# Dense expert scaling: the x input in two loads instead of three, and the first store tied to its own tile alone

## The chip, the cores and the metric

The kernel runs on one core of one Trainium2 chip. The metric is the device time in microseconds (us) of one execution; lower is better. Beside it stands the profile of one execution, whose span runs from the first to the last instruction of the core.

## What is computed

The inputs are `x`, 8 x 256 x 512 in float32 (4.19 MB), and `gate_weights`, 8 x 256 x 8 in float32. Each token's eight gate weights are divided by their sum, and each token's 512 values are multiplied by each of the eight results. The output is 8 x 256 x 8 x 512 in float32 (33.55 MB).

```python
gate_weights = gate_weights / (np.sum(gate_weights, axis=-1, keepdims=True) + 1e-8)
output = x[:, :, None, :] * gate_weights[:, :, :, None]
```

## The kernel before, in words

The 2048 tokens lie on 128 partitions, 16 consecutive tokens to a partition (`J` = 16), so that a token number j from 0 to 15 stands for 128 tokens, one per partition. All of x is kept on the chip in `x_all`, 32 KB a partition; one token j is 2 KB of a partition's row.

**Loads.** `first_load` (line 67, SP's queue) brings tokens 0 to 3, 8 KB a partition. `gate_load` (line 68, ACT's queue) brings all gate weights. `body_load` (line 69, SP) brings tokens 4 to 12, 18 KB a partition. These three are moved ahead of the barrier at the entry of the program, to the front of their engines' instructions, by `issue_before_entry_barrier`. The tail load (line 73, SP) brings tokens 13 to 15, 6 KB a partition, and is issued after that barrier.

**Gates.** Four small DVE instructions (lines 78 to 81) make the normalised gates `gn`.

**Products.** The results go into `ring`, ten slots of 16 KB a partition, one token j with its eight experts to a slot. `CHUNKS` lists the five stores as (first token, number of tokens, first slot): tokens 0-1 in slots 0-1, tokens 2-4 in slots 2-4, tokens 5-7 in slots 5-7, tokens 8-11 in slots 0-3, tokens 12-15 in slots 6-9. Slots 0 to 3 and 6 to 7 are used twice, so tokens 8 and 9 wait for store 0, tokens 10 and 11 for store 1, and tokens 12 and 13 for store 2. For tokens 0 and 1 ACT does three of the eight experts (line 88) and DVE five (line 90), one instruction to an expert; token 2 is all ACT's; of token 3 ACT does two and DVE six; tokens 5, 8 and 12 are all ACT's; each of the other tokens is one DVE instruction over all eight experts (line 93).

**Stores.** Each chunk ends in one DMA on SP's queue (line 118), which waits for the instructions that fill its slots. An extra dependency (lines 121 to 129) makes the first store wait for `body_load` too.

**Order.** Each engine takes its own instructions in order. The order in which the tokens of an engine stand is made by the framework's scheduler when the program is built, from the dependencies; it need not be the order of the source. SP issues all x loads and stores in one queue, and each DMA is spread over 16 DMA engines, 8 of the 128 partition rows to an engine. Nine DMAs are issued in all: three loads of x, one of the gates, five stores.

Of the kernel before, what the change touches and what calls it, by code (L numbers as in the profile page):

```python
# [1 line left out]

# [4 lines left out]

SLOTS = 10
HEAD = 4
TAIL = 13  # L10
CHUNKS = ((0, 2, 0), (2, 3, 2), (5, 3, 5), (8, 4, 0), (12, 4, 6))


def issue_before_entry_barrier(nc, loads):
    names = [bi.ins.name for bi in loads]

    def move(nc):
        blocks = nc.main_func.blocks
        entry = blocks[0].instructions
        moved = []  # L20
        for block in blocks[1:]:
            for ins in list(block.instructions):
                if ins.name in names:
                    block.instructions.remove(ins)
                    moved.append(ins)
        assert sorted(i.name for i in moved) == sorted(names)
        for ins in reversed(moved):
            at = next(k for k, other in enumerate(entry) if other.engine == ins.engine)
            entry.insert(at, ins)

    nc.at_finalize(move)


@with_exitstack
def kernel(
    ctx: ExitStack,
    tc: tile.TileContext,
    x: bass.AP,
    gate_weights: bass.AP,
    out: bass.AP,  # L40
):
    nc = tc.nc
    P = 128

    B, S, D = x.shape
    E = gate_weights.shape[-1]
    J = B * S // P

    fp32 = mybir.dt.float32
    mult = mybir.AluOpType.mult  # L50

    x_v = x.flatten_outer_dims().rearrange("(p j) d -> p j d", p=P)
    g_v = gate_weights.flatten_outer_dims().rearrange("(p j) e -> p j e", p=P)
    out_v = out.rearrange("b s e d -> (b s) e d").rearrange(
        "(p j) e d -> p j e d", p=P
    )

    pool = ctx.enter_context(tc.tile_pool(name="pool", bufs=1))

    g_all = pool.tile([P, J, E], fp32)  # L60
    x_all = pool.tile([P, J, D], fp32)
    ring = pool.tile([P, SLOTS, E, D], fp32)
    gsum = pool.tile([P, J, 1], fp32)
    gn = pool.tile([P, J, E], fp32)
    warm = pool.tile([P, 1], fp32)

    first_load = nc.sync.dma_start(out=x_all[:, 0:HEAD, :], in_=x_v[:, 0:HEAD, :])  # L67
    gate_load = nc.scalar.dma_start(out=g_all, in_=g_v)
    body_load = nc.sync.dma_start(
        out=x_all[:, HEAD:TAIL, :], in_=x_v[:, HEAD:TAIL, :]  # L70
    )
    issue_before_entry_barrier(nc, [first_load, gate_load, body_load])
    nc.sync.dma_start(out=x_all[:, TAIL:J, :], in_=x_v[:, TAIL:J, :])

    nc.vector.memset(warm, 0.0)  # L75
    nc.scalar.copy(out=warm, in_=warm)  # L76

    nc.vector.reduce_sum(out=gsum, in_=g_all, axis=mybir.AxisListType.X)  # L78
    nc.vector.tensor_scalar_add(out=gsum, in0=gsum, scalar1=1e-8)  # L79
    nc.vector.reciprocal(out=gsum, in_=gsum)  # L80
    nc.vector.tensor_tensor(  # L81
        out=gn, in0=g_all, in1=gsum.to_broadcast([P, J, E]), op=mult
    )

    def scale_one(engine, j, e, slot):
        o_ap, s_ap = ring[:, slot, e, :], gn[:, j, e : e + 1]
        if engine is nc.scalar:
            nc.scalar.mul(out=o_ap, in_=x_all[:, j, :], mul=s_ap)  # L88
        else:
            nc.vector.tensor_scalar_mul(out=o_ap, in0=x_all[:, j, :], scalar1=s_ap)  # L90

    def scale_token(j, slot):
        nc.vector.tensor_tensor(  # L93
            out=ring[:, slot, :, :],
            in0=x_all[:, j : j + 1, :].to_broadcast([P, E, D]),
            in1=gn[:, j, :].unsqueeze(2).to_broadcast([P, E, D]),
            op=mult,
        )

    for j0, m, s0 in CHUNKS:  # L100
        for i in range(m):
            j, slot = j0 + i, s0 + i
            if j < 2:
                for e in range(E):
                    on_act = e < 3
                    scale_one(nc.scalar if on_act else nc.vector, j, e, slot)
            elif j == 2:
                for e in range(E):
                    scale_one(nc.scalar, j, e, slot)
            elif j == 3:  # L110
                for e in range(E):
                    scale_one(nc.scalar if e < 2 else nc.vector, j, e, slot)
            elif i == 0:
                for e in range(E):
                    scale_one(nc.scalar, j, e, slot)
            else:
                scale_token(j, slot)
        store = nc.sync.dma_start(  # L118
            out=out_v[:, j0 : j0 + m, :, :], in_=ring[:, s0 : s0 + m, :, :]
        )  # L120
        if j0 == 0:
            tc.add_manual_dep(
                store.ins,
                body_load.ins.name,
                mybir.DependencyInfo(
                    mybir.DependencyClass.Sync, mybir.DependencyReason.DATA
                ),
                reason="no store among the loads",
            )


# [1 line left out]
_INS = ['x', 'gate_weights']  # L133
_OUTS = [((8, 256, 8, 512), 'float32')]


# [23 lines left out]
```

## Time and profile before

| what | value |
|---|---|
| median of 4 runs | 92.37 us (92.28 to 92.44) |
| the profiled execution's own time | 92.29 us |
| its span, first to last instruction | 90.5 us |
| DVE busy | 46.6 us (51%), 30 instructions |
| ACT busy | 26.3 us (29%), 42 instructions |
| DMA | 37.81 MB: 4.26 read from HBM, 33.55 written; 418 GB/s over the span |
| ACT waited for stores (line 88) | 25.0 us, in two waits |
| DVE waited for stores (line 93) | 3.7 us, in one wait |

The profile gives for each engine how long it was busy and what ended its idle time. DMA instructions appear twice: as issue on the queue's engine (SPq is SP's), which takes 0.33 to 0.42 us, and as landing, the time from the issue until the data's semaphore has arrived. Of the stores, store 0 was issued at 10.62 us from the span's start, store 1 at 17.15, store 2 at 25.82, store 3 at 47.50 and store 4 at 56.19; they landed 11.5, 19.4, 25.2, 22.9 and 33.5 us after their issues. A rate in GB/s is the bytes of the DMA packets recorded in a stretch.

### The profile page before, as it was taken

What the parts mean: (1) busy time and instruction counts of PE and PEld (TensorE: products, weight loads), DVE (VectorE), ACT (ScalarE), POOL (GpSimd) and SP (SyncE); (2) the same over time, 40 slices, a digit from 0 to 9 for tenths busy, and PEclk for the clock granted to TensorE, in tenths of its full rate; (3) what the DMA queues carried; (4) which work ended last, traced back from release to release, by engine and by line L of the source; (5) the groups of instructions that cost most, each with busy time, mean ns of one, the idle gap of its engine ahead of it and who ended that gap; (6) DMA issues with size and microseconds to landing.
All of it is one profiled execution on the core that took longest, in us unless ns stands there. A gap on an engine that the chain in (4) does not pass through costs nothing.

```text
span 90.5 us, 140 instructions
## 1 busy us (share of the span) xinstructions
DVE 46.6 (51%) x30; ACT 26.3 (29%) x42; POOL 0.2 (0%) x4
## 2 busy tenths in 40 slices
DVE  0069999999999999999990395000000000000000
ACT  4229999995990000000000398000000000000000
POOL 0000000000000000000000000000000000000000
DMA  5999999999898889888988999999999982999990
GB/s 127 470 417 399 415 518 463 463 420 391 348 695 348 348 348 695 348 348 348 695 348 348 463 463 463 463 463 463 463 463 463 463 377 87 463 463 463 463 463 0
DMA packets 1296, 37.81 MB, mean 418 GB/s; under 512 B 144, under 2 KB 272, under 8 KB 400
## 3 DMA queue, kind: packets, MB, share of 16 engines
q1 hardware_dynamic: 1152, 37.75, 97.2%
q10 hardware_dynamic: 144, 0.07, 0.2%
HBM read 4.26 MB, written 33.55 MB: 418 GB/s over the span
## 4 chain that ended last, share of the span: by engine, by line
DMA 52%; ACT 9%; ACTq 1%; SPq 0%; issue 0%
DMA out_dram<-ring 41%; DMA x_all<-in_x_dram 11%; ACT ring L88 9%; ACTq L155 1%; SPq L67 0%; ACTq L88 0%; SPq L118 0%
## 5 line engine op out<-in xcount | busy, mean ns | idle before, releaser
L93 DVE TENSOR_TENSOR ring<-x_all,gn 128x4096 f32<-128x4096 f32 x9 | 39.2, 4418 | 3.7 <-DMA out_dram<-ring 3.7
L88 ACT ACTIVATE ring<-x_all,gn 128x512 f32<-128x512 f32 x40 | 24.8, 708 | 28.6 <-DMA out_dram<-ring 25.0
L90 DVE TENSOR_SCALAR ring<-x_all,gn 128x512 f32<-128x512 f32 x16 | 6.4, 481 | 0.0
L78 DVE TENSOR_REDUCE gsum<-g_all 128x16 f32<-128x128 f32 x1 | 0.3, 285 | 3.8 <-DMA g_all<-in_gate_weights_dram 3.8
L76 ACT ACT_TABLE_LOAD x1 | 1.3, 1283 | 1.3 <-PEq L144 1.3
L75 DVE MEMSET warm<- 128x1 f32 x1 | 0.1, 59 | 1.3 <-PEq L144 1.3
L81 DVE TENSOR_TENSOR gn<-g_all,gsum 128x128 f32<-128x128 f32 x1 | 0.3, 291 | 0.0
L80 DVE RECIPROCAL gsum<-gsum 128x16 f32<-128x16 f32 x1 | 0.3, 253 | 0.0
L76 ACT COPY warm<-warm 128x1 f32<-128x1 f32 x1 | 0.2, 192 | 0.0
L79 DVE TENSOR_SCALAR gsum<-gsum 128x16 f32<-128x16 f32 x1 | 0.2, 174 | 0.0
L144 POOL MEMSET const-bfloat16-1.0<- 128x1 bf16 x1 | 0.1, 102 | 0.0
L144 POOL MEMSET const-uint8-127<- 128x1 uint8 x1 | 0.1, 102 | 0.0
L144 POOL MEMSET const-float32-0.0<- 128x1 f32 x1 | 0.1, 99 | 0.2 <-issue 0.2
L144 POOL MEMSET const-float32-1.0<- 128x1 f32 x1 | 0.1, 98 | 0.0
## 6 DMA issues: line engine op xcount, KB each, us to landing
out_dram<-ring SPq DMA_DIRECT2D x2, 6144.0 KB, 22.3
out_dram<-ring SPq DMA_DIRECT2D x1, 4096.0 KB, 11.5
x_all<-in_x_dram SPq DMA_DIRECT2D x1, 2304.0 KB, 10.1
x_all<-in_x_dram SPq DMA_DIRECT2D x1, 1024.0 KB, 5.0
x_all<-in_x_dram SPq DMA_DIRECT2D x1, 768.0 KB, 11.1
g_all<-in_gate_weights_dram ACTq DMA_DIRECT2D x1, 64.0 KB, 5.0
out_dram<-ring SPq DMA_DIRECT2D x2, 28.2
```

The costliest lines, as they stand in the source:

```text
L75: nc.vector.memset(warm, 0.0)
L76: nc.scalar.copy(out=warm, in_=warm)
L78: nc.vector.reduce_sum(out=gsum, in_=g_all, axis=mybir.AxisListType.X)
L79: nc.vector.tensor_scalar_add(out=gsum, in0=gsum, scalar1=1e-8)
L80: nc.vector.reciprocal(out=gsum, in_=gsum)
L81: nc.vector.tensor_tensor(out=gn, in0=g_all, in1=gsum.to_broadcast([P, J, E]), op=mult)
L88: nc.scalar.mul(out=o_ap, in_=x_all[:, j, :], mul=s_ap)
L90: nc.vector.tensor_scalar_mul(out=o_ap, in0=x_all[:, j, :], scalar1=s_ap)
L93: nc.vector.tensor_tensor(out=ring[:, slot, :, :], in0=x_all[:, j : j + 1, :].to_broadcast([P, E, D]), in1=gn[:, j, :].unsqueeze(2).to_bro ...
L144: nc = _bacc.Bacc("TRN2", target_bir_lowering=False, num_devices=1)
L155: with _tile.TileContext(nc) as tc:
```

## The change

The constant `TAIL` goes. The loads of tokens 4 to 12 and 13 to 15 become one load of tokens 4 to 15, 24 KB a partition, and it is among the three DMAs that are moved ahead of the entry barrier. The extra dependency of the first store is dropped. Eight DMAs remain. The products and the stores are written as before.

```diff
-TAIL = 13
...
-    body_load = nc.sync.dma_start(
-        out=x_all[:, HEAD:TAIL, :], in_=x_v[:, HEAD:TAIL, :]
-    )
-    issue_before_entry_barrier(nc, [first_load, gate_load, body_load])
-    nc.sync.dma_start(out=x_all[:, TAIL:J, :], in_=x_v[:, TAIL:J, :])
+    last_load = nc.sync.dma_start(out=x_all[:, HEAD:J, :], in_=x_v[:, HEAD:J, :])
+    issue_before_entry_barrier(nc, [first_load, gate_load, last_load])
...
-        store = nc.sync.dma_start(
+        nc.sync.dma_start(
             out=out_v[:, j0 : j0 + m, :, :], in_=ring[:, s0 : s0 + m, :, :]
         )
-        if j0 == 0:
-            tc.add_manual_dep(
-                store.ins,
-                body_load.ins.name,
-                mybir.DependencyInfo(
-                    mybir.DependencyClass.Sync, mybir.DependencyReason.DATA
-                ),
-                reason="no store among the loads",
-            )
```

## The prediction

> **What bounds the kernel now.** I read the DMA part of the page first, because the kernel moves 37.81 MB and computes little.
>
> ```profile
> GB/s 127 470 417 399 415 518 463 463 420 391 348 695 348 348 348 695 348 348 348 695 348 348 463 463 463 463 463 463 463 463 463 463 377 87 463 463 463 463 463 0
> q1 hardware_dynamic: 1152, 37.75, 97.2%
> q10 hardware_dynamic: 144, 0.07, 0.2%
> ```
>
> The 16 DMA engines carry packets for 97.2% + 0.2% of the 90.5 us span, 88.15 us. The remaining 2.4 us lie outside: nothing moves before 1.00 us (the row 0.50:1.00 below), and about 1.2 us at the end are the receipt of the last bytes and the final barrier (last landing 56.2 + 33.5 = 89.7, end 90.5). 1.0 + 88.15 + 1.2 = 90.35: there is practically no bubble inside. So a change pays only if it shortens the packets' own time, opens a bubble, or changes the first or the last microsecond.
>
> Second, the chain of waits, for the landings that follow each other:
>
> ```profile
> 0.43 10.10 DMA x_all<-in_x_dram
> ...
> 10.62 11.49 DMA out_dram<-ring
> ...
> 25.82 25.25 DMA out_dram<-ring
> ```
>
> Body load landed at 10.53, store 0 at 22.11, store 2 at 51.07; from the list of issues the tail load landed at 1.26 + 11.1 = 12.4 and store 4 at 89.7. From 22.11 to 51.07 the two 6.29 MB stores move 12.58 MB in 28.96 us, 434.5 GB/s; from 51.07 to 89.7 it is 16.78 MB in 38.6 us, 434 GB/s. Store 0 needs 4.19 MB / 434.5 = 9.65 us, and 22.11 - 9.65 = 12.46, the tail load's landing: it waited in the rings behind the loads.
>
> Third, whom the store queue waited for, and what ran when store 0 was issued:
>
> ```profile
> SPq L118 <- DVE ring L93: 43.4, 4, 21.3
> SPq L155 <- DMA out_dram<-ring: 32.9, 1, 32.9
> SPq L118 <- DMA x_all<-in_x_dram: 8.9, 1, 8.9
> ```
>
> ```profile
> 9.40 4.99 ACT L88 ACTIVATE ring<-x_all,gn 128x512 f32<-128x512 f32 x8
> 9.89 2.86 DVE L90 TENSOR_SCALAR ring<-x_all,gn 128x512 f32<-128x512 f32 x7
> 10.62 0.35 SPq L118 DMA_DIRECT2D out_dram<-ring  x1
> 12.66 4.42 DVE L93 TENSOR_TENSOR ring<-x_all,gn 128x4096 f32<-128x4096 f32 x1
> ```
>
> The 8.9 us wait for the body load is the one that the change removes. But what comes ready next is hardly earlier. DVE has 16 L90 instructions; 7 start from 9.89 on, so that one is the tenth, the last that DVE does for tokens 0 and 1, and it ends at 9.89 + 0.48 = 10.37. ACT's sixth starts at 9.40 and ends at 10.11. Store 0's own tile is ready at 10.37, against 10.53 for the body load.
>
> **The change part by part.** Durations are from the profiled execution (92.29 us, span 90.5, so 1.8 around it); the median of the runs is 92.37, and I apply the sum to that.
>
> *Store 0's wait removed.* Issue moves from 10.62 to 10.37 + 0.09 (the lag seen from 10.53 to 10.62) = 10.46, 0.16 us earlier. Price on the end: 0. The work that hides it is the loads still in the rings until about 12.0 (landing 12.4). In the trace's packet records (start and duration of each row on a DMA engine) store 0's first row starts at 11.585, 6 ns after that engine finished the tail load, the same 6 ns as at every later boundary, so its descriptors were waiting already. SP gains nothing either: store 1 waits for DVE's token 4 (17.15).
>
> *Two loads into one.* Each DMA is 128 rows, 8 to an engine. Per row the packet records give 309 ns for 8 KB, 234 ns for 6 KB, 686 for 18 KB, 1213 for 32 KB, 1815 for 48 KB. Body plus tail cost 686 + 234 = 920 ns. A 24 KB row does not occur; on the line between 18 KB and 32 KB it is 686 + 6144 x (1213 - 686) / 14336 = 912 ns. Saving 8 x 8 = 64 ns. One end-of-DMA record with its gaps (9 ns) goes too: 0.07 us together. Bounds: the loads between the landings 4.99 and 12.4 run at 3.146 MB / 7.41 us = 425 GB/s; at the stores' 434.5 they would take 7.24, so at best 0.17 us. At worst, the slowest of the 128 body rows took 787 ns; at that ratio a 24 KB row is 912 x 787/686 = 1046 and the load costs 8 x 126 - 9 = 1.0 us more. I take 0.07, as 126 of 128 rows took 686 exactly.
>
> *Issue ahead of the barrier.* SP's 0.33 us DMA instruction at 1.26 goes; the second load keeps its place at 0.43. The issue times (0.38, 0.42, 0.33, 0.35) don't grow with size, so the barrier should open at 1.26 as before. Price 0, because the tail load stood behind 3.3 MB anyway. The one thing it may touch is the slow start:
>
> ```profile
> 0.50:1.00 0.50, 0.00 (x0) 0.00 (x0) 0.00 (x0) 1.00 0.00 0
> 1.00:2.40 1.40, 0.06 (x1) 1.14 (x1) 0.00 (x0) 1.00 0.95 252
> 2.40:10.40 8.00, 5.08 (x15) 4.42 (x9) 0.00 (x0) 1.00 1.00 425
> ```
>
> From 1.00 to 2.40 the rate is 252 instead of 425 GB/s: (425 - 252) x 1.40 = 242 KB, worth 0.57 us. The tail's issue (1.26 to 1.59) falls into it. The first rows were slow from 1.01 on, before that issue, so I take 0; the bounds are -0.57 and, if a load twice as long crowds that start, about +0.3 (half of it).
>
> *A new wait.* Tokens 4 to 12 waited for the body load (10.53); all tokens from 4 up now wait for the whole load, 12.4 - 0.07 = 12.3. On DVE the first is token 4 (L93), and DVE is busy with L90 until 12.66: cover 0.3 us. Behind it stand tokens 6 and 7 and all later L93, and SP's store 1 waits for it. On ACT token 5 begins after 16 L88 instructions, 6.32 + 16 x 0.617 = 16.2. If the cover goes, store 1 is late; it was issued at 17.15, and needs about 1.0 us to its first byte as the first load did (issued 0.00, nothing before 1.00), 18.2 against the end of store 0's bytes near 21.7 (landing 22.11 less 0.4): 3.5 us more cover. The thinnest later one is store 3, issued at 47.50, ready by 48.5, against 50.7: 2.2 us. So a delay of DVE of up to 0.3 + 2.2 = 2.5 us costs nothing.
>
> The Trainium skill (Perfetto Trace Analysis, DMA Optimizations) speaks against the merger: smaller DMAs may let work start sooner, where DMA engines are generally idle. By it token 4 would lose 12.3 - 10.53 = 1.8 us, an estimate; the rows show DVE busy until 12.66 and no idle DMA, so I count 0. The skill (DMA: Bandwidth & Descriptors, Anatomy of one DMA) also states a fixed cost of about 2.0 us for each DMA on the GpSimd path; one DMA less would by that estimate end at 90.4, where the queued DMAs of this trace show 9 ns.
>
> *The end.* One semaphore fewer is waited for at the close; such waits last 17 to 27 ns, and some are done before the last landing. 0 to 0.03 us gained; I take 0.01.
>
> Sum: 0.00 + 0.07 + 0.00 + 0.00 + 0.01 = 0.08 us, 92.37 - 0.08 = 92.29. About 0.2% (0.18 us) is what a measurement of this kernel can tell from no change, so this is within it. Its own range is 92.15 (0.17 + 0.03 gained) to 92.45 (the scatter of the runs shown).
>
> **Rivals.**
> *A quicker start.* Without the post-barrier issue, part of the 0.57 us of slow start is recovered: half is 0.29, 92.29 - 0.29 = 92.0, all of it 91.7. For it: the low rate straddles the issue at 1.26 to 1.59. Against: the first rows are slow from 1.01 on.
> *A dearer long row* (slower). Place: the 24 KB load on the path between 4.99 and 12.4. It decides from 920 + 9/8 + 180/8 = 944 ns a row on, where the loss passes 0.18 us. If each row has the 787 ns row's ratio, 92.37 + 1.0 = 93.4; at a third of that excess 92.64. Against: one row of 128. The crowded start lies on the same side: 92.6.
> *Another order on DVE* (slower). The tokens are not computed in source order: eight L93 run without idle to 47.4, though tokens 10 and 11 need store 1 (landed 36.6), so tokens 14 and 15 went ahead of them. If the new waits put token 13 (which waits for store 2, 51.07) ahead of token 11, store 3 waits for 51.15 + 2 x 4.37 = 59.9, its bytes begin near 61, and the rings are empty from 50.7: +10 us, 102.7. With 14 and 15 behind 10 and 11 instead, store 3 goes out at 36.6 + 8.8 = 45.4 and nothing is lost. Against: 13 gets ready last in any order.
> *It doesn't do what it says*: store 0 finds its own tile as late as the load, and the rows cost the same: 92.37.
>
> **How the numbers follow.** Forecast 0.46 (0.40 within 0.2%, 0.06 below); no effect 0.07; quicker start 0.26 (0.24 faster); dearer row or crowded start 0.18, slower; another order 0.03, slower. So faster 0.30, within 0.49, slower 0.21. The predicted time is the forecast's, 92.29. The range goes down to 91.9, leaving out the fastest starts (about 0.08), and up to 92.8, leaving out long rows at full price and the other order (about 0.08). The likeliest case alone: 92.15 to 92.45.
>
> **What would show it.** Right: q1 1008 packets, last load landing at 12.3, store 0 issued near 10.46 and landing near 22.04, every later landing 0.07 earlier, DVE still without idle at 12.7, store 3 issued before 48. Wrong: a first x landing well off 5.0 (start), a last load landing after 12.5 (row), idle DVE between 12.7 and 47, or a landing-to-landing rate of the stores off 434 GB/s.

## The result, and the profile after

The changed kernel takes 92.24 us (median of 43 runs, 92.07 to 92.43); the kernel before, measured beside it, 92.35 us (63 runs, 92.22 to 92.58). The ratio is 0.9988 with a 95% interval of 0.9984 to 0.9993: 0.11 us less, between 0.06 and 0.15. That is a real gain, and a smaller one than the 0.2% that was named as the bound of what counts. The forecast was 0.08 us less.

The profiled execution of the changed kernel took 92.38 us, its span is 90.6 us; this one execution lies at the upper end of its 43 runs, above the profiled one of before. So the small gain can't be read from the two spans; single terms can. From the page's packets and DMA issues:

```profile
q1 hardware_dynamic: 1008, 37.75, 96.9%
q10 hardware_dynamic: 144, 0.07, 0.2%
...
out_dram<-ring SPq DMA_DIRECT2D x1, 4096.0 KB, 11.6
x_all<-in_x_dram SPq DMA_DIRECT2D x1, 3072.0 KB, 11.9
x_all<-in_x_dram SPq DMA_DIRECT2D x1, 1024.0 KB, 5.0
```

There are 144 packets fewer on SP's queue (128 rows and 16 end records), and the sum of their records, per DMA engine, falls from 87.93 us (97.2% of 90.5) to 87.82 (96.9% of 90.6). The merged load landed at 0.42 + 11.9 = 12.3 us, the tail load of before at 12.4.

The chain of waits has a new beginning (start, length, what):

```profile
6.32 4.06 DVE ring L86 x10
10.38 0.02 issue
10.40 0.02 SPq L114
10.42 0.04 issue
10.46 11.61 DMA out_dram<-ring
22.07 0.02 issue
...
25.83 25.27 DMA out_dram<-ring
```

Store 0 is released by the tenth product of DVE, at 10.38, and issued at 10.46 instead of 10.62. It lands at 22.07 instead of 22.11: its issue came 0.16 us earlier, its data only 0.04. Whom SP waited for:

```profile
SPq L114 <- DVE ring L89: 43.6, 4, 21.3
SPq L142 <- DMA out_dram<-ring: 33.0, 2, 19.2
SPq L114 <- DVE ring L86: 9.2, 1, 9.2
```

Where the body load stood (8.9 us) now stands DVE's own work (9.2 us): the wait changed its name, not its end. DVE shows no new idle time:

```profile
6.32 6.42 DVE L86 TENSOR_SCALAR ring<-x_all,gn 128x512 f32<-128x512 f32 x16
10.46 46.10 SPq L114 DMA_DIRECT2D out_dram<-ring  x5
12.66 34.77 DVE L89 TENSOR_TENSOR ring<-x_all,gn 128x4096 f32<-128x4096 f32 x8
```

Token 4 begins at 12.66, as before, 0.3 us after the merged load's landing. No bracket of idle time stands behind the eight instructions.

The trace's packet records (start and duration of each row on a DMA engine) give the last part. All 128 rows of 24 KB took 912 ns. On each DMA engine the first row of store 0 starts 6 ns after the start of the load's end record, 2 to 3 ns after the load's last row ended, as before. The 16 shares of the last store (one for each DMA engine) land at 89.43 on average (before 89.50), but from 89.24 to 89.78, spread over 0.53 us (before 0.26). The end waits for the latest of the 16. The spread begins with the first rows at 1.0 us, which take 0.3 to 1.3 us instead of 0.31, differently in every execution; this is why two single spans say nothing of 0.1 us. For the same reason the landings of whole stores are no earlier in this profile (store 2 at 51.11, before 51.07), while the means of their 16 shares are, by 0.02 to 0.07 us.

Two lengths do not depend on that start. The first is the stretch from the end of the first load to the end of the last load of x, as the mean of the 16 DMA engines: 7.325 us in this profile and in the four others below that keep this first load and the merged one (0.05 us of it is the gates' last row), 7.368 to 7.451 in the five profiles with three loads of x. Of the difference, 0.04 us is there even where no row was slow (7.368), and the rest, up to 0.08, comes with slow rows among the three loads. The second is the close. After the last landing the span goes on for 0.81 us, and for 0.85 before. SP steps there through its waits for the DMAs' semaphores in a fixed order: before, one more wait stood behind that for the last store, now none. It is 0.85 in all six profiles with nine DMAs, 0.81 in all five with eight, and 0.98 in the two with eleven and nineteen, where three waits stand behind it.

### The profile page after: what moved, and what is told of

It is laid out like the page before. It is cut to its first block, busy times and chain, and to the rows that moved or that the text cites. A ratio compares the mean times of both kernels' runs of the same rounds, so it can differ in the third digit from the quotient of the medians.

```text
span 90.6 us, 139 instructions
## 1 busy us (share of the span) xinstructions
DVE 46.6 (51%) x30; ACT 26.3 (29%) x42; POOL 0.2 (0%) x4
## 3 DMA queue, kind: packets, MB, share of 16 engines
q1 hardware_dynamic: 1008, 37.75, 96.9%
## 4 chain that ended last, share of the span: by engine, by line
DMA 46%; ACT 9%; DVE 6%; ACTq 1%; issue 0%; SPq 0%
DMA out_dram<-ring 41%; ACT ring L84 9%; DMA g_all<-in_gate_weights_dram 6%; DVE ring L86 4%; ACTq L142 1%; DVE gn L77 0%; DVE gsum L74 0%; DVE gsum L76 0%; DVE gsum L75 0%; ACTq L84 0%; SPq L114 0%
## 6 DMA issues: line engine op xcount, KB each, us to landing
x_all<-in_x_dram SPq DMA_DIRECT2D x1, 3072.0 KB, 11.9
```

## The experiments

The theory: the DMA rings (the rows queued on each DMA engine) are never empty, so only the time of the rows themselves counts, and the gain is that of one DMA and 128 rows fewer. The rivals: the wait held the stores back; the start is quicker without a DMA issue behind the barrier; the loads' number is worth far more (or nothing). Each kernel ran beside the kernel before.

**The wait alone.** The kernel before without its extra dependency:

```diff
-        if j0 == 0:
-            tc.add_manual_dep(
...
```

> Three loads of x as before; only the first store's wait for the body load is gone. Theory (the wait is covered by loads still in the rings): store 0 issued near 10.46 instead of 10.62 us, its landing unmoved near 22.1, time 92.35 us, ratio 1.000. Rival (the wait held the stores back, and its removal is the gain): the ratio of the whole change, 0.9988, about 92.24. Rival (a store among the loads costs): above 92.5.

Measured: 92.33 us, ratio 1.000 (0.9991 to 1.0009). Store 0 was issued at 10.48 and landed at 22.05. SP now waited for DVE instead of the load:

```profile
SPq L118 <- DVE ring L90: 8.8, 1, 8.8
```

Removing the wait shows no gain by itself. The interval shuts out the whole gain (0.9988), though not a part of it of up to 0.08 us.

**The place alone.** Three loads and the wait kept, the tail load moved ahead of the barrier too:

```diff
-    issue_before_entry_barrier(nc, [first_load, gate_load, body_load])
-    nc.sync.dma_start(out=x_all[:, TAIL:J, :], in_=x_v[:, TAIL:J, :])
+    tail_load = nc.sync.dma_start(out=x_all[:, TAIL:J, :], in_=x_v[:, TAIL:J, :])
+    issue_before_entry_barrier(nc, [first_load, gate_load, body_load, tail_load])
```

> Before, with its tail load issued ahead of the entry barrier too; wait and three loads kept. Theory (the place of the third issue is worth nothing): 92.35 us, first x landing at 5.0 us as before. Rival (a quicker start without the issue after the barrier): 92.0 to 92.25, the first x landing clearly before 4.9. Rival (three issues ahead delay the barrier by 0.4 us and that counts): above 92.5.

Measured: 92.38 us, ratio 1.0001 (0.9992 to 1.0009). The timeline shows what it moves:

```profile
0.89 0.43 SPq L72 DMA_DIRECT2D x_all<-in_x_dram  x1
1.72 1.28 ACT L76 ACT_TABLE_LOAD   x1 [1.72 <-PEq L144]
```

The barrier opens at 1.72 instead of 1.26, and nobody on the path waits for it. The first load landed at 4.9 (in the other profiles with the same first load, 4.9 to 5.1). The quicker start falls.

**The merged load, behind the barrier.** The other half of the same question:

```diff
-    last_load = nc.sync.dma_start(out=x_all[:, HEAD:J, :], in_=x_v[:, HEAD:J, :])
-    issue_before_entry_barrier(nc, [first_load, gate_load, last_load])
+    issue_before_entry_barrier(nc, [first_load, gate_load])
+    nc.sync.dma_start(out=x_all[:, HEAD:J, :], in_=x_v[:, HEAD:J, :])
```

> The changed kernel, with the merged load of twelve tokens issued after the entry barrier instead of ahead of it. Theory (the gain is that of one DMA and 128 rows fewer): as the changed kernel, 92.24 us, ratio 0.9988, last load landing near 12.3. Rival (the gain is that of the place): 92.35 or more.

Measured: 92.28 us, ratio 0.9991 (0.9983 to 1.0). The last load landed at 0.92 + 11.4 = 12.3. The gain is there without the place; its interval just touches 1, so taken alone it is weak, but with the two runs above, which show none, and the next two, where more loads cost more, it leaves the merger as the source.

**How much a row and a DMA cost.** Twelve tokens in four loads and in twelve, behind the barrier:

```diff
-    last_load = nc.sync.dma_start(out=x_all[:, HEAD:J, :], in_=x_v[:, HEAD:J, :])
-    issue_before_entry_barrier(nc, [first_load, gate_load, last_load])
+    issue_before_entry_barrier(nc, [first_load, gate_load])
+    for j in range(HEAD, J, 3):          # or 1
+        nc.sync.dma_start(out=x_all[:, j : j + 3, :], in_=x_v[:, j : j + 3, :])
```

> The changed kernel, with the twelve tokens in four loads of three tokens (6 KB rows), issued after the barrier. Theory (each row costs 7 ns beside its bytes, each DMA 9 ns): per DMA engine 4 x 8 x 234 + 4 x 9 = 7524 ns against 8 x 912 + 9 = 7305 for the one load, 0.22 us more than the changed kernel: 92.46, ratio 1.0012. Rival (about 2 us for each further DMA): 98. Rival (the number of loads is worth nothing, the gain came from elsewhere): 92.24.

> The changed kernel, with the twelve tokens in twelve loads of one token (2 KB rows), issued after the barrier. Theory: a 2 KB row costs about 83 ns on the line through the longer rows; per DMA engine 12 x 8 x 83 + 12 x 9 = 8076 ns against 7305, 0.77 us more: 93.0, last load landing near 13.1. Rival (about 2 us for each further DMA): above 110. Rival (worth nothing): 92.24.

Measured: four loads 92.62 us, ratio 1.0028 (1.0019 to 1.0037); twelve loads 93.74 us, ratio 1.0137 (1.0113 to 1.0161). Against the changed kernel's 92.24 that is 0.38 and 1.50 us, where 0.22 and 0.77 were expected. The direction and the order are the theory's, the sizes are not. The traces show what the theory left out.

For four loads the last store's shares land at 89.60 on average, 0.17 us later than in the changed kernel, and the close takes 0.98 us instead of 0.81. Together that is 0.33 of the 0.38 us; the rest is within the scatter.

For twelve loads the shares land at 90.24 on average, 0.81 later. That this meets the theory's 0.77 is partly luck: the 2 KB rows typically start 80 ns apart, which with 6 ns a load makes 12 x (8 x 80 + 6) = 7752 ns against 8 x 908 + 6 = 7270 for the one load, 0.48 us; the rest is mostly slower rows. Two thirds of the 2 KB records last 84 ns, most others 85 to 98, six of 1536 from 105 to 519. The slowest sets a single engine back: from the eighth load on the shares spread over 1.0 us instead of 0.5, and the engine never catches up. The latest share lands 0.68 us after the mean, at 90.92, where it was 0.34 in the changed kernel. The close again takes 0.98 us. The three, 0.81 + 0.34 + 0.17, make the 1.3 us between the two spans; the 1.50 between the medians is more because the profiled execution of the changed kernel lies 0.14 above its median.

The Trainium skill (DMA: Bandwidth & Descriptors, Anatomy of one DMA) states about 2.0 us fixed for each DMA on the GpSimd path. By it eleven DMAs more would be 22 us, an estimate; these eleven, queued behind each other on SP, cost 1.50 us in all, and the measurement decides.

**When a wait does cost.** The changed kernel, its first store waiting for the whole last load:

```diff
+        if j0 == 0:
+            tc.add_manual_dep(store.ins, last_load.ins.name, ...)
```

> The changed kernel, with the first store made to wait for the whole last load. Theory (a wait costs once the rings run dry): store 0 issued at 12.33 + 0.09 = 12.42 us, its first bytes some 0.97 later at 13.4, while the rings are empty from 11.5 to 11.95; about 1.4 us lost, 93.7, store 0 landing near 23.5. Rival (the queue hides an issue of this lateness): 92.3.

Measured: 93.94 us, ratio 1.0172 (1.0159 to 1.0185), 1.70 us above the changed kernel. DMA in three windows of this run (window, its length, DVE, ACT, POOL, clock, DMA share, GB/s):

```profile
11.00:12.00 1.00, 1.00 (x4) 1.00 (x3) 0.00 (x0) 1.00 0.01 0
12.00:13.00 1.00, 1.00 (x3) 1.00 (x3) 0.00 (x0) 1.00 0.00 0
13.00:13.40 0.40, 0.40 (x1) 0.40 (x2) 0.00 (x0) 1.00 3.05 1311
```

A packet counts whole in the window in which it starts, so the last rows of the load, which start before 11.00, do not show here, and a share can exceed 1. No row starts between 11.00 and 13.15. Store 0 was issued at 12.31, its rows start at 13.15 to 13.30, 0.84 us and more after the issue, on rings that had run dry from 11.53 to 11.81: a bubble of 1.5 us on average. After the bubble all 16 engines run in step, and the packet records show the stores' rows longer by 0.3 us in all (65,536 bytes in 2424 ns on average instead of 2420, the 32 KB rows 1224 instead of 1213), while the shares of the last store land closer together, within 0.20 us.

**How much cover DVE has.** Cover is the time by which something may come later without moving the end. DVE computes token 3's six products two and three times over:

```diff
                for e in range(E):
                    scale_one(nc.scalar if e < 2 else nc.vector, j, e, slot)
+                for _ in range(1):          # or 2
+                    for e in range(2, E):
+                        scale_one(nc.vector, j, e, slot)
```

> The changed kernel; DVE computes its six products of token 3 twice, which sets every later L93-type instruction back by 6 x 0.40 = 2.4 us. Theory (the thinnest later cover is that of store 3, about 2.1 us): store 3 issued at 49.9, first bytes near 50.9 against rings empty from 50.2 to 50.6: 0.2 to 0.4 us lost, 92.5. Rival (every microsecond of DVE counts): 94.6. Rival (more cover than read): 92.24.

> The changed kernel; DVE computes its six products of token 3 three times, 4.8 us later for what follows. Theory: store 3 issued at 52.3, first bytes near 53.3, rings empty from 50.6: about 2.6 us lost, 94.9. Store 1 issued near 22.0 also runs dry (rings empty from 21.15 to 21.6, first bytes near 22.9): 1.3 us of the loss comes there, and shifts the later landings, so that store 3 loses the rest, 1.3. Rival (the cover is all one needs up to 5 us): 92.24.

Measured: 92.63 us, ratio 1.0027 (1.0017 to 1.0038), and 95.02 us, ratio 1.0283 (1.0268 to 1.0297): 0.39 and 2.78 us above the changed kernel, 0.26 and 2.66 expected. The windows around store 3 in the shorter delay:

```profile
49.50:50.30 0.80, 0.47 (x1) 0.00 (x0) 0.00 (x0) 1.00 0.00 0
50.30:50.80 0.50, 0.00 (x0) 0.00 (x0) 0.00 (x0) 1.00 0.02 0
50.80:51.60 0.80, 0.35 (x1) 0.36 (x1) 0.00 (x0) 1.00 3.07 1311
```

Store 3 was issued at 50.0, its rows start at 50.87 to 51.02, on rings that ran dry from 50.32 to 50.78. In the longer delay the packet records show two bubbles, at store 1 (dry from 21.19 to 21.66, rows from 22.88) and at store 3 (52.0 to 52.16, rows from 53.20), 1.5 and 1.2 us. A delay of 2.4 us of DVE costs 0.4, one of 4.8 costs 2.8: the first two microseconds are free, and beyond them each costs about one.

**Two other cuts.** Three loads without the wait, cut 6 + 6 and 3 + 9 tokens instead of 9 + 3:

```diff
-TAIL = 13
+TAIL = 10          # or 7
```

> The kernel with three loads and without the store's wait, cut 6 + 6 tokens instead of 9 + 3. By the bytes and rows alone two 12 KB rows cost 2 x 460 = 920 ns, as 18 KB + 6 KB do (686 + 234): 92.33, ratio 1.000. In the profiles with 18 KB rows a dozen of them ran 10 to 200 ns longer between 5.6 and 7.3 us, while no 24 KB row did. If that comes with the size of 18 KB, it is gone here, 0.03 to 0.05 us less; if it comes with the stretch of time or with shorter rows, some 12 KB rows between 5.6 and 7.3 us are slow too.

> The kernel with three loads and without the store's wait, cut 3 + 9 tokens instead of 9 + 3: the 18 KB rows begin only at about 6.2 us. By rows and bytes: 92.33, ratio 1.000. If the slow rows belong to the size of 18 KB, they are seen later, from the second row on; if to the stretch from 5.6 to 7.3 us, some of the rows running then, 6 KB or 18 KB, are slow.

Measured: 92.33 us, ratio 0.9998 (0.9989 to 1.0008), and 92.38 us, ratio 1.0004 (0.9991 to 1.0016). Where three loads are cut makes no difference that can be told. All 256 rows of 12 KB took 460 ns, while with 3 + 9 a dozen 18 KB rows took up to 898 ns instead of 686, from 7.3 us on. So the slow rows came with the 18 KB rows and not with the stretch of time; but in two of the three profiles cut 9 + 3 a few 6 KB rows behind them were slow too (four and six, up to 334 ns instead of 234), so it is not the size of the slow row alone. The 18 KB rows add 47 ns to a DMA engine on average here, and in the four profiles that have them 8 to 60. How much of the gain they are is open: the cut without them is no faster, but its interval of 0.09 us to either side could not show it.

**A try at the slow start.** The first load cut in two, one half on ACT's queue:

```diff
-    first_load = nc.sync.dma_start(out=x_all[:, 0:HEAD, :], in_=x_v[:, 0:HEAD, :])
+    first_load = nc.sync.dma_start(out=x_all[:, 0:2, :], in_=x_v[:, 0:2, :])
+    second_load = nc.scalar.dma_start(out=x_all[:, 2:HEAD, :], in_=x_v[:, 2:HEAD, :])
```

> The changed kernel, with its first load cut in two: tokens 0 and 1 on SP's queue, tokens 2 and 3 on ACT's queue ahead of the gates, both at the very start. In the profiles the first row of each DMA engine takes 0.5 to 1.3 us instead of 0.31, some 0.5 us lost on each. If that loss is the delay of one queue's first row, two queues side by side hide part of it: 0.2 to 0.4 us less, 91.9 to 92.05. If it is the memory or the engine itself: 128 more rows and one more DMA cost 8 x 7 + 9 = 65 ns, 92.3, ratio 0.9995; the gates land later, which nothing waits for until the rings run dry.

Measured: 99.64 us, ratio 1.0784 (1.0769 to 1.0799), which met neither expectation. The start was not quicker (last load landed at 0.42 + 12.0 = 12.4), and the sentence that nothing waits for the gates fell:

```profile
0.53 0.45 ACTq L68 DMA_DIRECT2D g_all<-in_gate_weights_dram  x1
...
12.61 0.29 DVE L75 TENSOR_REDUCE gsum<-g_all 128x16 f32<-128x128 f32 x1 [11.08 <-DMA g_all<-in_gate_weights_dram]
...
17.89 45.68 SPq L115 DMA_DIRECT2D out_dram<-ring  x5
```

The gates landed at 0.53 + 12.06 = 12.6 instead of 5.2, and store 0 went out at 17.89. With two queues busy, each DMA engine takes a row of one and a row of the other in turn: the gates' eight 512-byte rows now alternate with eight rows of 24 KB (the packet records have them from 4.93 to 11.92 us, one every 0.93 us on a DMA engine), where before they alternated with the first load's 8 KB rows. The Trainium skill (DMA: Bandwidth & Descriptors, Queues, rings and completion order) states such a turn by turn between queues, packet by packet, with some 9 to 17 descriptors to a packet; here the turn is taken after every single row.

No version was found that beats the changed kernel.

## Why the prediction was right

*The bound.* Right. What lay under the rings' cover did not count, and every bubble showed in the time (0.4, 1.7 and 2.8 us, made on purpose, and 7.4 us with the late gates). What was left to gain was the rows' own time and the close.

*The wait removed, priced 0.* Right, by the run with that edit alone (1.000). Store 0's own tile was ready at 10.38, read beforehand as 10.37; its issue at 10.46 came as worked out. The 6 ns that the prediction reads from the end of the load to the first row of store 0 run from the start of the end record; from the end of the last row it is 2 ns, which only strengthens the reading that the store was waiting.

*One load for two, priced 0.07.* Right in kind: the 24 KB row was put at 912 ns on the line through the neighbours, and took 912; the merger alone gave 0.9991. The size was too high. A row starts some 4 ns before the record of the row ahead of it ends: 24 KB rows follow each other every 908 ns, 18 KB rows every 682, 6 KB rows every 230 to 231. So a pair of rows made into one saves 4 to 5 ns and not 8, and the end of a DMA costs 6 ns and not 9. Together that is 0.04 us, as the three loads without a slow row show (7.368 against 7.325 us). The slow rows of the three loads, 0.01 to 0.08 us, had been seen as two of 128 and left out. The rate bound of 0.17 us gave the range its lower end, and was not reached.

*Issue ahead of the barrier, priced 0.* Right (1.0001). Its reason was right too: two DMAs on SP stand ahead of the barrier before and after, and it opened at 1.26 and 1.25.

*The new wait, priced 0.* Right: token 4 began at 12.66. The cover at store 3 was read as 2.2 us and measured as 2.0 (2.4 us of delay cost 0.39). The lead from issue to first byte was taken as 1.0 from the first load; on rings run dry it is 0.84 to 0.99.

*The end, 0.01.* Too low, and its bounds of 0 to 0.03 as well: the close is 0.04 us shorter in every profile with eight DMAs than in every one with nine.

*The sum.* The measured 0.11 us has an interval of 0.06 to 0.15, so the sum of 0.08 can't be told from it. That the sum fits so well is partly luck: 0.07 + 0.01 was forecast where the traces show 0.04 + 0.04, and the slow rows come on top. What it also left out is that the end is that of the latest of 16 DMA engines, not of their mean.

*The rivals.* The quicker start fell by two runs. The dearer long row fell: none of 128 was slow, and in the five other profiles with 24 KB rows none took over 914 ns. Another order on DVE did not come: each engine has the same groups in the same places. The case without effect falls by the interval.

## What to carry to other kernels

Where every store is issued before the rings run dry, a wait, a barrier or a late landing is free up to the cover, and each microsecond beyond it costs one: read the cover as the time from issue to the end of the bytes queued ahead, less about 1 us until the first byte. Under that cover, only the number of rows and DMAs remains to be saved, and it is small: here 4 to 5 ns a row and 6 ns a DMA on each DMA engine, some 0.04 to 0.06 us for each wait at the close that stands behind the last store's, and more when slow rows scatter the engines. Take the cost of a row from the starts of two rows that follow each other, not from the length of one record. Before a small load is put on another queue, look at what size of row it will take turns with.

## What the runs showed of the hardware that was not expected

- With two queues busy a DMA engine takes turns row by row: eight rows of 512 bytes beside rows of 24 KB landed at 12.6 us, beside rows of 8 KB at 5.2.
- The 16 DMA engines land their shares of the first load over 0.3 to 0.6 us and mostly keep that spread to the end. In the four profiles with a bubble, where the shares then land within 0.2 us, the stores' rows are longer: 2423 to 2427 ns on average for 64 KB instead of 2418 to 2422 in the others. That the one causes the other is not shown.
- In all four profiles with 18 KB rows some of these took 700 to 900 ns instead of 686, two rows in one, a dozen or more in the others; rows of 12 KB and 24 KB never did. The cause is open.
- The close after the last landing took 0.81, 0.85 or 0.98 us, with none, one or three of SP's waits behind that for the last store.
- Each DMA that SP issues ahead of the entry barrier holds the barrier back: it opened at 0.91 us with one, 1.25 to 1.26 with two and 1.72 with three.
